# mLSTM's q, k, gate and value projections as seven half-size products each

## The chip, the cores and the metric

The kernel runs on one core of a Trainium2 chip. The metric is the device time of one execution in microseconds. Before the change the median of three runs is 1254.02 us (1248.43 to 1255.01).

## What is computed

One decoder layer on x of 1024 tokens x 1024 features, in float32. A normalised x goes through one projection `w_in`. It feeds eight dilated attention heads and four mLSTM heads; their outputs meet in `w_out`, and a gated convolutional FFN of width 2816 follows. What matters here is the part of the projection that feeds the mLSTM heads:

```python
def _hybrid_mixer(h, w_in, ...):
    proj = h @ w_in
    aq, ak, av, mq, mk, mv, mo, mig, mfg = jnp.split(proj, SPLITS, axis=-1)
    ...
    mqk = jax.nn.silu(_causal_dwconv(jnp.concatenate([mq, mk], axis=-1), mlstm_conv_w, mlstm_conv_b))
    mq, mk = jnp.split(mqk, 2, axis=-1)
    ...
    hm = _mlstm_chunkwise(ml_heads(mq), ml_heads(mk) * (MLSTM_HEAD_DIM ** -0.5), ml_heads(mv), log_i, log_f)
    hm = _rmsnorm(hm, ...)
    hm = jax.nn.sigmoid(mo.astype(jnp.float32)) * hm
```

q, k, the gate `mo` and the values `mv` are 512 columns each; the gate unit also carries the eight columns of the input and forget gates.

## The kernel before

Every float32 product is three matmuls of rounded parts: high by high, high by low, low by high (`mm3`, L327). An operand is therefore split into a high part (a rounded copy, on ACT or VectorE) and a low part (a subtraction, on VectorE or POOL).

The program is one long instruction list for each engine, written out by a planner. `Clock` (L29) holds a modelled time for each engine, `Lanes` (L171) a list of generators with priorities. A generator yields what it needs (tiles, free pages of SBUF, free PSUM banks, a condition), and the planner goes on with the first lane whose needs are met at TensorE's modelled time. The order on each engine is fixed by this plan; on the chip each instruction waits for its semaphores in that order. The planner's `dma` (L291) counts loads on SP's queue one after the other and does not count transfers that other engines issue.

x is kept as sixteen pages, `xh` and `xl`, high and low part of eight blocks of 128 features by 1024 tokens. The first three q and k units are multiplied while x arrives (the loop at L504), 18 matmuls for each block. `project` (L648) then goes through `order` (L404): the units m (q or k of a head, `ml_conv` behind each), g (gate), v (mLSTM values), a (attention values) and h (q and k of an attention head). An m or h unit is 2 halves of tokens x 8 blocks x 3 matmuls of 512 columns. A g or v unit is 8 token blocks x 8 feature blocks x 3 matmuls of 260 or 256 columns. The gate stays in SBUF (`sg`), as do q and k (`qk`). `mlstm` (L810) runs a head's recurrence over eight chunks when its q, k, values and gates are there. In the same stretch run the attention lanes `scores`, `trans` and `values` (L943 to L1039).

`stacks` (L912) prepares an attention head: it scales the product by R, splits it, and swaps halves of 64 partitions between three pages with four transfers SBUF to SBUF (`move`, L306, on SP's queue):

```python
        move(kS[lo, A], q2[up, A])
        move(kS[up, A], q1[up, A])
        move(q1[up, A], q2[lo, A])
        move(q2[up, A], q1[lo, A])
```

The FFN already uses seven products of half size for each 2 x 2 block product. The sums of its weights are made in DRAM by `sums` (L788): a copy issued on ACT's queue, then an add issued on POOL's queue (`accum_op`), each of 5.6 MB for the upward weights, planned from 70 us on at intervals of 55 us.

Of the kernel before, what the change touches and what calls it, by code (L numbers as in the profile page):

```python
# [223 lines left out]
def tile_hybrid_layer(ctx, tc, xT, x, w_t, w_v, w_g, w_o, w_uq, w_dq, params, fnw, c_id, c_att, c_sel,  # L224
# [14 lines left out]
    usum = {p: dram.tile([DFF, 512], F32, name=f"usum{p}") for p in (3, 5, 6, 7)}  # L239
    hpark = [dram.tile([128, 1024], F32, name=f"hpark{i}") for i in range(8)]  # L240
# [65 lines left out]
    def move(dst, src):  # L306

        nc.sync.dma_start(f32(dst), f32(src))
        t = max(clk.eng.get("dma", 1.7), clk.ready(src), clk.last(dst))
        clk.eng["dma"] = t + 0.7  # L310
        for a in (dst, src):
            n = a.tensor.name
            clk.acc[n] = max(clk.acc.get(n, 0.0), clk.eng["dma"] + 2.0)
        for k in clk.cells(dst):
            clk.wr[k] = clk.eng["dma"] + 2.0
            clk.weng[k] = "dma"
# [19 lines left out]
    class Feed:  # L336
# [35 lines left out]
        def split_next(self):  # L372
            n, raws = self.raw.pop(0)
            res = []
            for raw, s in zip(raws, self.units[n]):
# [4 lines left out]
                e = dve if hold or clk.eng.get("pool", 0.0) > clk.eng.get("dve", 0.0) + PB else pool  # L380
                e.tensor_tensor(lo[:, :w], raw[:, :w], f32(hi[:, :w]), op=OP.subtract)
# [22 lines left out]
    order = "m3 g0 g1 v0 m4 m5 v1 m6 m7 a0 h0 h1 h2 h3 a1 h4 h5 h6 h7"  # L404
    for o in order.split():
        n = int(o[1])
        if o[0] == "m":
            unit("ml", n, [w_t[n]])
        elif o[0] == "h":
            unit("att", n, [w_t[8 + n]])  # L410
        elif o[0] == "g":
            unit("g", n, [w_g[n, 0], w_g[n, 1]])
        elif o[0] == "v":
            unit("mv", n, [w_v[2 + n, 0], w_v[2 + n, 1]])
        else:
            unit("av", n, [w_v[n, 0], w_v[n, 1]])
    feed = Feed(units, 1, 6)
# [23 lines left out]
    xh = [page(f"xh{k}", F32R) for k in range(8)]  # L441
    xl = [page(f"xl{k}", F32R) for k in range(8)]
    w0 = [page(f"w0r{c}") for c in range(3)]
    w0h = [page(f"w0h{c}", F32R) for c in range(3)]
    w0l = [page(f"w0l{c}", F32R) for c in range(3)]
    raws = {}
    H = [slice(0, 512), slice(512, 1024)]

    def load_x(k, hf):
        if hf == 0:  # L450
            raws[k] = page("xr")
        dma(raws[k][:, H[hf]], xT[k * 128:(k + 1) * 128, H[hf]])

    def load_w0(k, n):
        sl = slice(k * 128, (k + n) * 128)
        for c in range(3):
            dma(w0[c][:, sl], w_t[c][:, sl])

    def load_nat(i):
        t = page("xnat")  # L460
        dma(t[:, :D], x[i * 128:(i + 1) * 128, :])
        raws["n", i] = t

    def split_x(k, hf):
        wn = pr[:, P_XN + k:P_XN + k + 1]
        xr = raws[k]
        act.activation(xh[k][:, H[hf]], xr[:, H[hf]], AF.Copy, scale=wn)
        dve.scalar_tensor_tensor(xl[k][:, H[hf]], xr[:, H[hf]], wn, f32(xh[k][:, H[hf]]), op0=OP.mult,
                                 op1=OP.subtract)
        if hf:  # L470
            free(raws.pop(k))

    def split_w0(k, n):
        sl = slice(k * 128, (k + n) * 128)
        for c in range(3):
            dve.tensor_copy(w0h[c][:, sl], w0[c][:, sl])
            pool.tensor_tensor(w0l[c][:, sl], w0[c][:, sl], f32(w0h[c][:, sl]), op=OP.subtract)

# [29 lines left out]
    for k in range(8):  # L508
# [4 lines left out]
        elif k + 2 < 8:  # L513
            if k == 2:
                load_w0(4, 4)
            load_x(k + 2, 0)
            load_x(k + 2, 1)
        if k == 4:
            feed.fetch(0)
            dma(ident, c_id)  # L520
            for i in range(4):
                load_nat(i)
# [1176 lines left out]
```

## Time and profile before

| | us |
|---|---|
| median of 3 runs | 1254.02 |
| lowest, highest | 1248.43, 1255.01 |
| the profiled execution | 1251.1 |
| its span, first to last instruction | 1249.3 |
| TensorE busy | 1221.0 |
| VectorE busy | 868.2 |
| ACT busy | 576.5 |
| POOL busy | 300.0 |

Busy times are unions of an engine's instructions; waiting and issuing transfers are not counted. The ends of matmuls are modelled, so the pace from one start to the next says more than the busy time. Nearly all instructions carry line L153, a helper that records them; they are told apart by the names of what they write and read. The granted clock of TensorE over the span is 0.99 of full speed.

### The profile page before, as it was taken

Reading aid. Unit: us, or ns where it says so; the run is one execution under the profiler, and the core shown is the slowest. Engines: PE = TensorE matmul, PEld = TensorE weight load, DVE = VectorE, ACT = ScalarE, POOL = GpSimd, SP = SyncE. Lnnn points to the kernel's source line nnn. Section 1 sums busy time; section 2 is a strip of 40 time slices with the busy share of each in tenths; the row PEclk is TensorE's granted clock in tenths of the full one; section 3 lists DMA queues with packets and bytes.
Section 4 is the critical chain, followed back from the end, with each engine's and each line's share of the span. In section 5 each row is a group of like instructions: output and inputs, shape, how many; then the busy total and the mean of one; then the engine's idle time right before and its main releaser. Section 6 shows DMA issues by size and latency. Waiting matters only on the chain. (4 is left out here: it accounts for less than half of the span.)

```text
span 1249.3 us, 17498 instructions
## 1 busy us (share of the span) xinstructions
PE 1221.0 (98%) x6366; PEld 1031.3 (83%) x6366; DVE 868.2 (69%) x1622; ACT 576.5 (46%) x1146; POOL 300.0 (24%) x213
## 2 busy tenths in 40 slices
PE   9999999999999699999999999999999999999997
PEld 6899898988998598788878888888888888888886
DVE  6733472657784487635799877777776878877865
ACT  4454554536562366334654344343343444343553
POOL 3420132121103103121133332323322222424002
PEclk9999999999999799999999999999999999999999
DMA  9460656668493759823663865546634279433334
GB/s 332 174 213 25 147 163 231 144 152 251 129 193 94 269 178 233 214 86 142 143 212 133 243 222 164 188 161 195 179 107 152 82 288 409 148 102 90 97 97 147
DMA packets 66366, 216.41 MB, mean 173 GB/s; under 512 B 7268, under 2 KB 8804, under 8 KB 61288
## 3 DMA queue, kind: packets, MB, share of 16 engines
q1 hardware_dynamic: 61032, 146.09, 34.8%
q0 software_dynamic: 4352, 34.60, 13.7%
q10 hardware_dynamic: 896, 34.60, 8.1%
q8 instruction: 50, 0.82, 0.3%
q14 instruction: 36, 0.29, 0.1%
HBM read 182.76 MB, written 93.32 MB: 221 GB/s over the span
## 5 line engine op out<-in xcount | busy, mean ns | idle before, releaser
L153 PE MATMUL bank<-xb,W 128*128 128x512 f32 x1848 | 431.1, 395 | 2.6 <-POOL W L153 2.1
L153 PEld LDWEIGHTS bank<-xb,W 128*128 128x128 f32 x1848 | 347.8, 188 | 84.9 <-POOL W L153 2.5
L153 PE MATMUL bank<-B,A 128*128 128x512 f32 x924 | 214.0, 394 | 0.0
L153 PEld LDWEIGHTS bank<-B,A 128*128 128x128 f32 x924 | 173.6, 188 | 40.2
L153 POOL TENSOR_TENSOR W<-ur,W 128x512 fp32r<-128x512 f32 x82 | 107.2, 1329 | 278.4 <-ACT W L153 258.0
L153 ACT ACTIVATE ua<-bank,pr 128x512 f32<-128x512 f32 x84 | 63.0, 777 | 168.9 <-DVE bank L153 161.0
L153 DVE SCALAR_TENSOR_TENSOR ua<-bank,pr,ua 128x511 f32<-128x511 f32 (+1 forms) x168 | 125.4, 746 | 15.9 <-ACT ua L153 12.9
L153 DVE TENSOR_TENSOR bank<-bank,ut 128x512 f32<-128x512 f32 x84 | 58.6, 697 | 38.2 <-PE bank L153 37.2
L153 ACT ACTIVATE W<-ur 128x512 fp32r<-128x512 f32 x133 | 78.5, 623 | 5.9 <-DMA ur<-in_w_uq_dram 3.2
L153 ACT ACTIVATE A<-g 128x512 fp32r<-128x512 f32 x76 | 47.3, 627 | 71.9 <-DVE g L153 47.2
L153 DVE CUSTOM_DVE_ANT_0 P<-bank,matt 128x512 f32<-128x512 f32 (+3 forms) x96 | 50.7, 552 | 19.6 <-PE bank L153 17.5
L153 ACT ACTIVATE P<-P,nmx 128x128 f32<-128x128 f32 (+3 forms) x64 | 49.5, 773 | 29.3 <-DVE nmx L153 29.0
L153 DVE TENSOR_TENSOR ut<-ut,bank 128x512 f32<-128x512 f32 x66 | 45.0, 681 | 19.5 <-PE bank L153 19.0
L153 DVE TENSOR_TENSOR B<-br,B 128x512 fp32r<-128x512 f32 x67 | 50.4, 755 | 11.5 <-ACT B L153 11.4
L153 DVE TENSOR_TENSOR PT<-bank,PT 128x512 fp32r<-128x512 f32 (+1 forms) x80 | 48.3, 630 | 8.2 <-ACT PT L153 7.9
L153 PE MATMUL bank<-kS,q 128*128 128x512 f32 (+3 forms) x192 | 42.4, 354 | 10.9 <-DMA q<-q 10.9
L153 POOL TENSOR_TENSOR A<-g,A 128x512 fp32r<-128x512 f32 x17 | 23.2, 1372 | 122.2 <-ACT A L153 122.2
L153 DVE TENSOR_TENSOR W<-ur,W 128x512 fp32r<-128x512 f32 x72 | 49.9, 701 | 2.2 <-ACT W L153 1.5
L153 DVE TENSOR_TENSOR A<-g,A 128x512 fp32r<-128x512 f32 x60 | 41.7, 700 | 13.6 <-ACT A L153 13.2
L153 DVE TENSOR_TENSOR hq<-hq,bank 128x512 f32<-128x512 f32 x56 | 34.9, 681 | 20.9 <-PE bank L153 20.9
L153 ACT ACTIVATE B<-br 128x512 fp32r<-128x512 f32 x69 | 42.4, 619 | 14.9 <-DMA br<-in_w_dq_dram 10.1
L153 ACT ACTIVATE PT<-bank 128x512 fp32r<-128x512 f32 (+1 forms) x71 | 36.5, 547 | 24.9 <-PE bank L153 23.4
(357 smaller groups left out, 2467.2 us busy)
## 6 DMA issues: line engine op xcount, KB each, us to landing
usum<-in_w_uq_dram POOLq DMA_DIRECT2D x4, 5632.0 KB, 34.9
ur<-usum SPq DMA_DIRECT2D x88, 256.0 KB, 4.5
ur<-in_w_uq_dram SPq DMA_DIRECT2D x66, 256.0 KB, 4.6
usum<-in_w_uq_dram ACTq DMA_DIRECT2D x2, 5632.0 KB, 21.1
usum<-usum ACTq DMA_DIRECT2D x2, 5632.0 KB, 22.8
tsum<-in_w_dq_dram POOLq DMA_DIRECT2D x4, 2816.0 KB, 18.1
gp<-ua SPq DMA_DIRECT2D x22, 512.0 KB, 2.9
g<-gp SPq DMA_DIRECT2D x22, 512.0 KB, 7.6
```

What stands on the lines that cost most here:

```text
L153: r = f(*a, **k)
```

## The change

Each of the four projections is cut in two along features and in two along tokens or columns, and its four quarter results are put together from seven products of half size. x becomes blocks `xp[1]` to `xp[7]` of 512 features by 512 tokens: the quarters for products 1 to 3, sums for 5 to 7 and 4, made by `x_half` and `x_sums`. The weight sums for products 3, 5, 6 and 7 are made in DRAM by `p_sums`, by a copy on ACT's queue and an add on POOL's queue each, at times of the plan that `p_plan` lists. `products` runs the steps: q and k of four heads with products 1 and 2, the gate with 1 and 2, the gate's rest in the order 6, 7, 5, 3, 4, q's and k's rest for two heads at a time, then the values. `m_evac` and `t_evac` combine the results on VectorE. q and k after the convolution (`qkp`) and the gate (`gpark`) are stored to DRAM on POOL's queue and loaded again by `mlstm`. `project` keeps the attention units alone, and starts behind the last product; the second token half of the first four x blocks is loaded and split again for it (`x_last`, `xp[8]`). The half swaps of `stacks` go to POOL's queue (`put`). The FFN's upward sums move from 70 us, every 55, to 130 us, every 40.

```diff
+    gpark = dram.tile([128, 8, 512], F32, name="gpark")
+    msum = {p: dram.tile([512, 512], F32, name=f"msum{p}") for p in (3, 5, 6, 7)}
+    gsum = {p: dram.tile([128, 1040], F32, name=f"gsum{p}") for p in (3, 5, 6, 7)}
+    vsum = {p: dram.tile([128, 1024], F32, name=f"vsum{p}") for p in (3, 5, 6, 7)}
+    qkp = [dram.tile([128, 1024], F32, name=f"qkp{i}") for i in range(8)]
...
-    def move(dst, src):
-        nc.sync.dma_start(f32(dst), f32(src))
...
+    def put(dst, src):
+        nc.gpsimd.dma_start(dst, src)
+        t = max(clk.eng.get("pool", 0.0), clk.ready(src), clk.last(dst))
+        clk.eng["pool"] = t + 1.0
         for a in (dst, src):
             n = a.tensor.name
-            clk.acc[n] = max(clk.acc.get(n, 0.0), clk.eng["dma"] + 2.0)
-        for k in clk.cells(dst):
-            clk.wr[k] = clk.eng["dma"] + 2.0
...
-    order = "m3 g0 g1 v0 m4 m5 v1 m6 m7 a0 h0 h1 h2 h3 a1 h4 h5 h6 h7"
+    order = "a0 h0 h1 h2 h3 a1 h4 h5 h6 h7"
...
-    feed = Feed(units, 1, 6)
+    feed = Feed(units, 1, 6, wait=lambda: "plain" in flags)
...
+    xs = [page(f"xs{k}") for k in range(8)]
+    xp = {p: {} for p in range(1, 9)}
+    wn = lambda k: pr[:, P_XN + k:P_XN + k + 1]
+    rest = (6, 7, 5, 3, 4)
+    psteps = [("m", h, p) for p in (1, 2) for h in range(4)] + [("g", 0, 1), ("g", 0, 2)]
+    psteps += [("g", 0, p) for p in rest]
+    psteps += [("m", h, p) for i in (0, 2) for p in rest for h in (i, i + 1)]
+    psteps += [("v", 0, p) for p in (1, 2) + rest]
+    praw, pw = {}, {}
+    pused = [0]
+    sumt = {}
...
     dma(pr, params)
-    load_x(0, 0)
-    load_w0(0, 1)
...
-    rst_pg = page("rst")
-    rst = rst_pg[0:4, :S]
-    for k in range(8):
...
+    for k in (0, 4, 1, 5, 2, 6, 3, 7):
+        dma(xs[k][:, U], xT[k * 128:(k + 1) * 128, U])
+    def p_load():
+        n = 8
+        while n < len(psteps):
+            m = psteps[n][0] == "m"
+            yield need(pg=1, keep=2, cond=lambda: n < max(pused[0] + (5 if m else 3), 11) and summed(n))
+            if m:
+                yield need(pg=1, keep=2, cond=lambda: summed(n + 1))
+            t = page("pr")
+            for j in range(1 + m):
+                src = psrc(*psteps[n + j])
+                dma(t[:, H[j]] if m else t[:, :src.shape[-1]], src)
+                praw[n + j] = t
+            n += 1 + m
...
+    def p_side():
+        for n, (u, h, p) in enumerate(psteps):
+            m = u == "m"
+            yield need(cond=lambda: n in praw and n < pused[0] + (4 if m else 3 if n < 11 else 2))
+            r = praw.pop(n)
...
+                    yield from split(t, r[:, H[i]])
+                if i:
+                    free(r)
...
+    def x_half(p, k, hf, raw):
+        s_ = xs[k][:, H[hf]]
+        if raw:
+            yield need(s_, pg=1)
+            t = page(f"xp{p}", F32R)
+            act.activation(t[:, L], s_, AF.Copy, scale=wn(k))
+            yield need(t[:, L])
+            dve.scalar_tensor_tensor(t[:, U], s_, wn(k), f32(t[:, L]), op0=OP.mult, op1=SUB)
+            xp[p][k % 4] = t
+            yield need(t, cond=lambda: len(xp[2]) == 4)
+            act.activation(s_, s_, AF.Copy, scale=wn(k))
+        else:
+            yield need(s_)
+            act.activation(s_, s_, AF.Copy, scale=wn(k))
+            if p:
+                flags.add(("x", k, hf))
+                yield need(s_, pg=1, keep=2, cond=lambda: len(xp[5]) > k - 4 and calm())
+                t = page(f"xp{p}", F32R)
+                yield from split(t, s_)
+                xp[p][k % 4] = t
+        flags.add(("x", k, hf))
...
+    def x_sums(f):
+        yield need(cond=lambda: all(("x", k, hf) in flags for k, hf in ((f, 0), (f, 1), (f + 4, 0), (f + 4, 1))) and calm())
+        lo, up = xs[f], xs[f + 4]
+        yield need(lo, up, pg=1)
+        tm = page("xt")
+        two(lo[:, U], lo[:, U], lo[:, L], SUB)
+        yield need(lo)
+        two(tm[:, L], up[:, U], lo[:, U], SUB)
+        for p, src in ((6, tm[:, L]), (7, tm[:, U]), (5, lo[:, U]), (4, up[:, L])):
+            if p == 7:
+                two(tm[:, U], tm[:, L], lo[:, L], SUB)
+                two(up[:, L], up[:, L], tm[:, L], SUB)
+            yield need(src, pg=1, cond=calm)
+            t = page(f"xp{p}", F32R)
+            yield from split(t, src)
+            xp[p][f] = t
+            if p in (5, 7):
+                free(lo if p == 5 else tm)
+            before = {6: 6, 7: 7, 5: 3, 4: 3}[p]
+            yield need(cond=lambda: len(xp[before]) == 4)
+        free(up)
...
+    def p_sums(u, quarters, into, plan_):
+        for t, to, src, add in plan_:
+            yield need(cond=lambda: clk.eng.get("pe", 0.0) > t)
+            src = quarters[src] if isinstance(src, tuple) else into[src]
+            if add:
+                nc.gpsimd.dma_start(into[to], src, accum_op=ADD, max_dma_last_dim=8192)
+            else:
+                nc.scalar.dma_start(into[to], src)
+            if add:
+                sumt[u, to] = clk.eng["pe"] + 10.0
+    def p_plan(c, a, c6, a6, c3, a3):
+        return ((c, 5, (1, 0), 0), (c, 7, (1, 0), 0), (a, 5, (1, 1), 1), (a + 1, 7, (0, 0), 1), (c6, 6, 5, 0),
+                (a6, 6, (0, 0), 1), (c3, 3, 6, 0), (a3, 3, (0, 1), 1))
+    ij = [(i, j) for i in range(2) for j in range(2)]
+    lanes.add(p_sums("g", {k: w_g[k] for k in ij}, gsum, p_plan(11, 17, 23, 29, 35, 41)), 0.1)
+    lanes.add(p_sums("m", {k: w_mq[k].rearrange("h p c -> (h p) c") for k in ij}, msum, p_plan(20, 30, 40, 48, 57, 65)), 0.2)
+    lanes.add(p_sums("v", {k: w_v[2 + k[0], k[1]] for k in ij}, vsum, p_plan(36, 44, 52, 60, 68, 74)), 0.3)
...
+        put(qkp[2 * h + isk], a[:, :S])
...
+    def m_evac(h, p, b):
+        if p == 1:
+            yield need(b, pg=1 - h % 2)
+            if h % 2 == 0:
+                run[h] = page("ut")
+            t = run[h // 2 * 2][:, H[h % 2]]
+            act.activation(t, b, AF.Copy)
+            run["m", h] = t
+            freebank(b)
+            return
+        yield need(b, cond=lambda: ("m", h) in run)
+        t = run["m", h]
+        yield need(t, pg=1 if p in (2, 7) else 0)
+        if p == 2:
+            zt[h, 0] = page("z0")
+            dve.tensor_tensor(zt[h, 0][:, L], b, t, op=ADD)
+            flags.add(("C", h, 0, 0))
+            flags.add(("at", h, 2))
+            freebank(b)
+            return
+        yield need(cond=lambda: ("at", h, {6: 2, 7: 6, 5: 7, 3: 5, 4: 5}[p]) in flags)
+        if p == 6:
+            dve.tensor_tensor(t, t, b, op=SUB)
+        elif p == 7:
+            zt[h, 1] = page("z1")
+            dve.tensor_tensor(zt[h, 1][:, L], t, b, op=ADD)
+        elif p == 5:
+            dve.tensor_tensor(zt[h, 0][:, U], t, b, op=SUB)
+            dve.tensor_tensor(zt[h, 1][:, U], b, zt[h, 1][:, L], op=SUB)
+            flags.add(("C", h, 1, 1))
+            if ("at", h ^ 1, 5) in flags:
+                free(run[h // 2 * 2])
+        elif p == 3:
...
+                    put(gpark[:, 2 * i:2 * i + 2, :], sg[i][:, :S].rearrange("p (t c) -> p t c", t=2))
...
+    def products():
+        for n, (u, h, p) in enumerate(psteps):
+            if u != "m" and p == 2:
+                yield need(pg=2)
+                dst = sg if u == "g" else va
...
+                for t in va[-2:]:
+                    pool.memset(t[:, :1032].rearrange("p (t h j) -> p t h j", t=2, h=4)[:, :, :, 128:129], 1.0)
+            yield need(cond=lambda: n in pw)
+            w = pw[n]
+            if u == "m":
+                yield need(*w, bk=1, kb=2)
+                b = bank("fg")
+                for f in range(4):
+                    yield need(cond=lambda: f in xp[p])
+                    x_ = xp[p][f]
+                    yield need(x_)
+                    fs, fl = slice(f * 128, (f + 1) * 128), slice(512 + f * 128, 512 + (f + 1) * 128)
+                    mm3(b, w[0][:, fs], w[0][:, fl], x_[:, L], x_[:, U], f == 0, f == 3)
+                lanes.add(m_evac(h, p, b), 3)
+            else:
...
+                    if u == "g" or j % 2 == 0:
+                        yield need(*w, bk=1, kb=2)
+                        b = bank("fg")
+                    o = b[:, :c] if u == "g" or j % 2 == 0 else b[:, 256:512]
+                    for f in range(4):
+                        yield need(cond=lambda: f in xp[p])
+                        x_ = xp[p][f]
+                        yield need(x_)
+                        fs = slice(f * c, (f + 1) * c)
+                        mm3(o, x_[:, j * 128:(j + 1) * 128], x_[:, 512 + j * 128:512 + (j + 1) * 128], wh[:, fs],
+                            wl[:, fs], f == 0, f == 3)
+                    if u == "g" or j % 2:
+                        lanes.add(t_evac(u, p, j if u == "g" else j // 2, b), 3)
+            free(*pw.pop(n))
+            pused[0] = n + 1
+            if u == "v" and p in (4, 5, 6, 7):
+                free(*xp.pop(p).values())
+            if n == len(psteps) - 3:
+                flags.add("plain")
+        flags.add("products")
...
-    lanes.add(sums(70, 55, uq, usum, ((5, (1, 0), 0), (5, (1, 1), 1), (6, 5, 0), (6, (0, 0), 1), (3, 6, 0),
+    lanes.add(sums(130, 40, uq, usum, ((5, (1, 0), 0), (5, (1, 1), 1), (6, 5, 0), (6, (0, 0), 1), (3, 6, 0),
...
     def mlstm(h):
-        yield need(cond=lambda: 2 * h in qk and 2 * h + 1 in qk and "urow" in G and ("mv", h // 2) in flags)
-        q, k = qk.pop(2 * h), qk.pop(2 * h + 1)
+        yield need(pg=2, keep=5, cond=lambda: 2 * h in qk and 2 * h + 1 in qk and "plain" in flags
+                   and (h == 0 or ("begun", h - 1) in flags))
+        q, k = page("q"), page("k")
+        for i, t in enumerate((q, k)):
+            dma(t[:, :S], qkp[2 * h + i])
+        yield need(q, k, pg=1, keep=5, cond=lambda: "urow" in G and "v" in flags)
+        flags.add(("begun", h))
         urow = G["urow"]
-        yield need(q, k, pg=1, keep=5)
...
+        dma(yp[:, :S].rearrange("p (t c) -> p t c", t=8), gpark[:, :, h * 128:(h + 1) * 128])
...
-        move(kS[lo, A], q2[up, A])
-        move(kS[up, A], q1[up, A])
-        move(q1[up, A], q2[lo, A])
-        move(q2[up, A], q1[lo, A])
+        put(f32(kS[lo, A]), f32(q2[up, A]))
+        put(f32(kS[up, A]), f32(q1[up, A]))
+        yield need(kS)
+        put(f32(q1[up, A]), f32(q2[lo, A]))
+        put(f32(q2[up, A]), f32(q1[lo, A]))
```

## Rows read from the trace of the kernel before

**Rows 1.** the page: each engine's busy us, share and instructions

```profile
PE 1221.0 (98%) x6366; PEld 1031.3 (83%) x6366; DVE 868.2 (69%) x1622; ACT 576.5 (46%) x1146; POOL 300.0 (24%) x213
```

**Rows 2.** TensorE's waits, whole span: us in total, times, longest

```profile
PE bank L153 <- DMA q<-q: 10.9, 2, 8.9
...
PE bank L153 <- DVE W L153: 0.4, 1, 0.4
```

**Rows 3.** groups of instructions (busy us, mean ns), then two stretches (header above)

```profile
L153 PE MATMUL bank<-xb,W 128*128 128x512 f32 x1848 | 431.1, 395 | 2.6 <-POOL W L153 2.1 <-DVE W L153 0.4
...
core 0: us, PE busy (x) PEld busy (x) DVE busy (x) ACT busy (x) POOL busy (x), PEclk, DMA share, GB/s
80.00:100.00 20.00, 20.00 (x169) 20.00 (x169) 0.00 (x0) 4.32 (x15) 0.00 (x0) 1.00 0.67 215
...
56.00:66.00 10.00, 10.00 (x86) 10.00 (x85) 10.00 (x8) 6.59 (x8) 2.13 (x1) 1.00 0.15 52
```

**Rows 4.** TensorE in order of time, 8 to 20 us: start, us, instructions

```profile
10.97 0.94 PE L153 MATMUL bank<-xh,w0h 128*128 128x512 f32 x3 [1.26 <-DVE w0h L153]
17.66 0.51 PE L153 MATMUL bank<-xh,w0l 128*128 128x512 f32 x1 [0.63 <-POOL w0l L153]
```

**Rows 5.** stretches, same columns: two early ones, a copy, adds, adds with loads

```profile
0.00:5.00 5.00, 3.81 (x9) 1.34 (x10) 0.76 (x6) 2.21 (x3) 0.66 (x5) 1.00 0.52 159
20.00:40.00 20.00, 20.00 (x88) 16.19 (x87) 14.79 (x17) 9.63 (x15) 9.84 (x6) 1.00 1.03 413
75.00:80.00 5.00, 5.00 (x44) 5.00 (x44) 0.00 (x0) 2.58 (x5) 4.09 (x5) 1.00 1.06 364
605.00:615.00 10.00, 10.00 (x45) 8.12 (x44) 9.79 (x18) 6.56 (x13) 1.57 (x1) 1.00 1.01 210
485.00:515.00 30.00, 28.23 (x176) 24.30 (x174) 19.31 (x53) 14.30 (x32) 0.00 (x0) 1.00 1.03 247
```

**Rows 6.** groups by shape: VectorE whole span, then ACT from 0 to 165

```profile
L153 DVE TENSOR_TENSOR ut<-ut,bank 128x512 f32<-128x512 f32 x66 | 45.0, 681 | 19.5 <-PE bank L153 19.0
L153 DVE TENSOR_TENSOR OT<-bank,osum 64x256 f32<-64x256 f32 x32 | 13.3, 414 | 7.5 <-ACT osum L153 6.6
L153 DVE SCALAR_TENSOR_TENSOR xl<-xr,pr,xh 128x512 fp32r<-128x512 f32 x16 | 14.7, 954 | 7.7 <-ACT xh L153 7.7
...
L153 ACT ACTIVATE w1h<-wr 128x1040 fp32r<-128x1040 f32 x2 | 2.1, 1074 | 2.9 <-DMA wr<-in_w_g_dram 2.9
```

**Rows 7.** the stretch from 0 to 163; groups of it by shape

```profile
0.00:163.00 163.00, 158.52 (x1030) 140.57 (x1031) 84.35 (x126) 83.80 (x181) 42.93 (x32) 0.99 0.58 180
...
L153 DVE SCALAR_TENSOR_TENSOR mqk<-mz,pr,mqk 128x1023 f32<-128x1023 f32 x5 | 10.5, 2109 | 0.0
L153 DVE SCALAR_TENSOR_TENSOR mqk<-mz,pr,mqk 128x1021 f32<-128x1021 f32 x4 | 5.1, 1274 | 0.0
```

**Rows 8.** in order of time, 405 to 435 us; then the stretch at its end

```profile
408.34 0.50 ACTq L799 DMA_DIRECT2D usum<-in_w_uq_dram  x1
...
427.74 0.48 PE L153 MATMUL bank<-kS,q 128*128 128x128 f32 x1 [8.89 <-DMA q<-q]
430.22 1.65 PE L153 MATMUL bank<-kS,q 128*128 128x128 f32 x5 [2.00 <-DMA q<-q]
...
430.00:435.00 5.00, 4.78 (x13) 4.09 (x14) 2.61 (x12) 0.49 (x2) 0.00 (x0) 0.50 0.19 76
```

**Rows 9.** DMA issues: KB each, us to landing; POOL's issue; fifth head in time

```profile
usum<-in_w_uq_dram POOLq DMA_DIRECT2D x4, 5632.0 KB, 34.9
kS<-q SPq DMA_DIRECT2D x16, 256.0 KB, 3.6
...
L796 POOL DMA_DIRECT2D usum<-in_w_uq_dram x4: 1132/1172/1291, 133.4 to 480.4; - x4
...
397.80 1.10 SPq L308 DMA_DIRECT2D q<-q  x2
...
403.71 0.98 PE L153 MATMUL bank<-kS,q 128*128 128x128 f32 x6
```

More of the change, by code (lines that the diff above doesn't have):

```diff
@@ new lines, in calm, with stats @@
+    def calm():
+        return max(clk.eng.get("dve", 0.0) - 2.5, 1e-9)
+    for k in range(4):
+        lanes.add(x_half(1, k, 0, True), 2.0)
+    for k in range(4, 8):
+        lanes.add(x_half(2, k, 0, True), 2.1)
+    for k in range(4):
+        lanes.add(x_half(0, k, 1, False), 2.2)
+        lanes.add(x_half(3, k + 4, 1, False), 2.25)
+        lanes.add(x_sums(k), 2.3)
+    def stats():
+        for i in range(8):
+            yield need(pg=1, keep=4, cond=lambda: len(xp[2]) == 4 and len(stat_done) > i - 3)
+            t = page("xnat")
+            dma(t[:, :D], x[i * 128:(i + 1) * 128, :])
+            lanes.add(stat(i, t), 2.6)
+        dma(ident, c_id)
+        dma(tri, c_tri)
+        yield need(ident, cond=lambda: len(stat_done) == 8)
+        dve.tensor_scalar(ss, ss, 1.0 / D, EPS, op0=OP.mult, op1=OP.add)
+        pool.tensor_tensor(rn, ss, half, op=OP.pow)
+        yield need(rn, pg=1)
+        R.append(page("R"))
+        for hf in range(2):
+            yield need(bk=1)
+            pR = bank()
@@ L619, in tile_hybrid_layer @@
     va = []
-    vap = []
     av = {}
@@ new lines, in x_last @@
+    def x_last():
+        for f in range(4):
+            yield need(pg=2, cond=lambda: 5 not in xp)
+            r = page("xr")
+            dma(r[:, L], xT[f * 128:(f + 1) * 128, U])
+            t = page("xp8", F32R)
+            yield need(r)
+            act.activation(t[:, L], r[:, L], AF.Copy, scale=wn(f))
+            yield need(t[:, L])
+            dve.scalar_tensor_tensor(t[:, U], r[:, L], wn(f), f32(t[:, L]), op0=OP.mult, op1=SUB)
+            free(r)
+            xp[8][f] = t
+    lanes.add(x_last(), 2.3)
@@ L648, in project @@
     def project():
+        yield need(cond=lambda: "products" in flags)
         for n, (kind, arg) in enumerate(plan):
@@ L874, in mlstm @@
             free(ET, ST)
-        free(q, k, vap[h])
+        free(q, k)
+        flags.add(("vused", h))
+        if all(("vused", j) in flags for j in range(4)):
+            free(*va)
         yield need(nmp, pg=1)
@@ L943, in scores @@
     def scores():
+        yield need(pg=1, cond=lambda: "products" in flags)
+        matt = page("matt")
+        dma(matt[:, :S], c_att)
+        yield need(matt)
         for h, pr_ in pairs:
@@ L1239, in tile_hybrid_layer @@
     gp = [dram.tile([128, 1024], F32, name=f"gp{k}") for k in range(NK)]
-    L, U = slice(0, 512), slice(512, 1024)
-    ADD, SUB = OP.add, OP.subtract
-    def two(out_, a, b, op):
-        end = {}
-        for n in ("dve", "pool"):
-            c = clk.cost(n, "tensor_tensor", [out_], [a, b], {})
-            end[n] = clk.start(n, c, [out_], [a, b]) + c
-        (pool if end["pool"] + 0.3 < end["dve"] else dve).tensor_tensor(out_, a, b, op=op)
-    def split(t, src):
-        copy(t[:, L], src)
-        yield need(t[:, L])
-        two(t[:, U], src, f32(t[:, L]), SUB)
     def blocks_ready(hf):
```

428 lines of the change are left out of this document (239 added, 189 removed).

## Prediction

> **What bounds the kernel now.** I read the busy shares first, then what TensorE waits for, then the stretches. TensorE is busy 98% of the span, every other engine 69% or less [rows 1]. That alone proves little, since the ends of matmuls are modelled, so the second view counts: all waits of TensorE that the trace names, ten rows, come to about 22 us, and 10.9 us of them are two waits for the half-swapping transfers of one attention head [rows 2]. The third view is the pace. 1848 matmuls of 512 columns with no others between take 431.1 us, 0.233 us each; in a stretch of value products 169 matmuls of 256 columns fill 20 us, 0.118 us each; in a gate stretch 86 fill 10 us, some of them cut by its edges, 0.12 us for 260 columns [rows 3]. So the kernel's time is its number of matmul columns plus some 25 us of holes. A matmul that goes saves its whole pitch, if what is left stays fed.
>
> **The change, part by part.** *Products.* Before, the eight q and k units take 2 halves x 8 blocks x 3 = 48 matmuls of 512 each (384), the two gate units 8 x 8 x 3 = 192 of 260 each (384), the two value units as many of 256. After, q and k are 4 head groups x 7 products x 4 blocks x 3 = 336, gate and value 7 x 4 x 4 x 3 = 336 each. 48 go of each kind: 48 x 0.233 + 48 x 0.12 + 48 x 0.118 = 22.6 us. All of it is on TensorE, so all of it is on the path. Transposes, attention, output and FFN keep their counts.
>
> *The start.* Before, 144 products need 33.5 us and run from 5 to 42 us: 3.5 us of waits, seen as the two gaps at 11 and 17.7 us [rows 4]. The new start asks for the same first 256 KB of x and 64 KB of weights; I let its own waits cost the same 3.5 us.
>
> *The sums of weights.* Each of gate, q/k and value gets four copies (ACT's queue) and four adds (POOL's queue) in DRAM: 2.1 + 4.2 + 2.1 = 8.4 MB copied and 8.4 MB added, planned between 11 and 74 us. Rates, each from a stretch with that traffic alone: loads 413 GB/s, a copy 364, an add 210, all three at a full DMA share; an add with loads beside it moves 247 in all [rows 5]. The eight p1 and p2 steps of q and k keep TensorE from 5 to 5 + 96 x 0.233 = 27.4 us. By then the first gate weights must be in. In front of them on SP's queue lie 24 half blocks of 256 KB, with the gate page 6.8 MB: 16.5 us, and some 3 us more because the first 5 us moved only 159 GB/s [rows 5]. The sums planned before 27 us bring copies of 3.7 MB (10.2 us) and adds of 1.06 MB (5.1 us). Together the engines need until 35 us, and the split of the page takes 1.07 us on ACT and, at twice 0.68, about 1.4 on VectorE [rows 6]: some 10 us late. The lower bound is 0, if the loads win the sharing; the upper is +20, if the q/k adds (2.1 MB, 10 us) also get in front. The early stretch of before is nearest: with loads alone it waited 3.5 us at a full share. I take +7, range -3 to +23. Two blocking points add to the upper end: a copy waits in ACT's stream for the add it reads, with evacuations and splits behind it, and an add waits in POOL's stream for its copy, with weight splits and the new stores behind it.
>
> *VectorE.* Added in the first 163 us, at about 0.7 us for 512 columns [rows 6]: evacuations of q/k 28 x 0.69, less nothing, because the 16 multiplications by R remain (19 us); of gate and value 28 x 0.42 (as for 256 columns) + 14 x 0.69 = 21; x splits and sums 20 x 0.7 + 16 x 0.69 + 4 x 0.95, less 8 x 0.95 = 21; 12 more pages of weight splits at 1.4 = 17. That is 78 us, and the last two convolutions, some 12 us, come in, while about 25 us of gates and recurrences move behind. VectorE has 84 us and POOL 43 us there now [rows 7]; with POOL's time at half, 106 + 78 + 12 - 25 = 171 us of VectorE's work in about 160. POOL can take 30 or 40 of it. VectorE stays under the bound as a mean, but the q/k stretch holds 48 us of convolutions beside 17 of evacuation in 56 us, and it must spill into the value stretch. An operation can get longer there: the convolution's step of 1023 columns takes 2.11 us in the mean of this stretch, its step of 1021 columns 1.27 [rows 7]. I take +3, range 0 to +15 if that cover fails.
>
> *Attention's transfers.* The four half swaps of a head go from SP's queue to POOL's. Now, at 408.34 us ACT issues a 5.6 MB copy; TensorE then stands 8.89 and 2.00 us for swaps, and has half its clock from 430 to 435 us, 1.2 GHz after 10 us of standing still: 10.9 + 2.5 = 13.4 us [rows 8]. A swap lands in 3.6 us normally [rows 9]. The FFN's sums move to 130 us and every 40 us, so copies and adds cover the attention stretch as densely as now. Best case: no swap meets one, -13. Worst: two heads sit behind whole adds, 34.9 us each [rows 9], less 6 us from the last swap to the scores (397.80 to 403.71 for the fifth head) [rows 9]: 2 x 29 - 13.4 = +44. The nearest row is that one head's stall, which a new spacing moves but does not remove: 0.
>
> *Parking and reloads.* q, k and gate make 6.3 MB of stores and as many loads in 1249 us; POOL's issues, 12 stores and 32 swaps at about 1.2 us, as its adds take now [rows 9], are 53 us on an engine that is 24% busy. The recurrences ask for them when two value products are still to run, and a0, h0 to h2 lie behind as cover. Nothing; a few us, if a load meets a 5.6 MB copy.
>
> Sum: -22.6 + 7 + 3 + 0 = -12.6. The profiled execution took 1251.1 us (1.8 around its span), 2.9 below the median: 1238.5 on its scale, 1241.4 on the median's. I say 1240. All terms at their ends at once would give 26 less or 72 more.
>
> **The rivals.** *All fed, 1226.* The gate weights come in time and the new spacing spares the swaps half of their 13.4 us: 1254 - 22.6 - 6 = 1226. For it: the adds are needed late, the value sums only after 124 us. Against it: the full DMA share of the early stretch even without sums [rows 5].
>
> *Swaps queue behind adds, 1266, slower.* A POOL queue that takes swaps after a 5.6 MB add in the order of issue lets them land when the add has. Place: the heads from h3 on, whose scores follow the last swap as closely as the fifth head's. Price: 20 us for each of two heads, 40 in place of 13.4, so 1240 + 27 = 1266. It decides from one head that waits 26 us in all. The adds fill 35 of each 80 us, so of five heads two are exposed. Against it: heads stacked early have other attention work in front of them. The Trainium skill, "DMA: Bandwidth & Descriptors", section "Queues, rings and completion order", says that a DMA engine takes its queue rows in turn, packet by packet, and consumes one row's descriptors in ring order. The stretch with an add and loads agrees on the turns (247 GB/s against 210); no row shows a transfer behind an add in its own queue. By that rule a swap on SP's queue shares with an add, and one on POOL's waits for its end: it is this rival.
>
> *The sums starve the loads throughout, 1256.* Up to the last gate product (67 us): 8.4 MB of adds 40 us, 8.4 of copies 23, 14.2 MB of loads 34, 97 us against some 75: 22 us late instead of 7, so 1240 + 15 = 1255 to 1257.
>
> *VectorE sets the pace, 1252.* +15 instead of +3.
>
> *The change doesn't cut the columns.* Excluded by the counts above.
>
> **How the numbers follow.** Forecast 1240 (its own range 1232 to 1248): 0.42. All fed: 0.22. Swaps behind adds: 0.17. Sums starve: 0.11. VectorE: 0.08. About 0.5%, 6.3 us, is what a measurement of this kernel can tell from no change: 1247.7 to 1260.3. Faster: 0.39 of the forecast's share and 0.22, 0.61. Same: 0.03 of the forecast, 0.08, and 0.07 of the starving case, 0.18. Slower: 0.17 and 0.04, 0.21. The range 1224 to 1266 leaves out the better end of the second case and the worse end of the third, under 0.2.
>
> **What would show it.** Right: 336 products each; a TensorE gap of 5 to 10 us before the first gate product at about 27 us; VectorE over 80% busy from 40 to 160 us; the first out-projection product some 10 us earlier than now. Wrong upward: no gap there and TensorE's waits under 15 us in all. Wrong downward: a wait on kS or q1 of over 15 us beside an add, or TensorE waiting for summed weights after 70 us.

## The result, and the profile after

The kernel after takes 1369.71 us (median of 4 runs, 1368.39 to 1371.01), the kernel before 1251.94 (median of 4 beside them): a ratio of 1.094, with an interval of 1.091 to 1.098. The change costs 117.8 us; 1240 was forecast, 1266 was the upper end.

The page of after, the rows that answer to [rows 1], and the granted clock and the DMA share in 40 slices of 34 us (tenths):

```profile
PE 1228.4 (90%) x6222; PEld 1031.6 (75%) x6222; DVE 934.9 (68%) x1759; ACT 604.6 (44%) x1197; POOL 266.8 (19%) x239
...
PEclk9789988889798999799999999999999999999999
DMA  9987579465979377922154756665563358733324
```

144 matmuls fewer, as the change says, and TensorE's busy share falls from 98% to 90%. No other engine is near its bound. The clock drops in some of the first 17 slices and nowhere behind them. TensorE's waits answer to [rows 2] (us in total, times, longest); two rows of POOL's and one of SP's queue stand below them:

```profile
PE bank L153 <- DMA q<-q: 43.5, 6, 19.0
PE bank L153 <- DVE rows L153: 17.8, 2, 17.3
PE bank L153 <- ACT pwh L153: 17.6, 2, 14.1
PE bank L153 <- DVE y L153: 10.9, 2, 10.2
PE bank L153 <- ACT PT L153: 8.5, 1, 8.5
...
POOL q L313 <- DMA kS<-q: 77.1, 7, 33.0
POOL gsum L675 <- DMA gsum<-gsum: 21.8, 2, 17.7
...
SPq L297 <- DMA y<-gpark: 29.2, 1, 29.2
```

Some 22 us of waits have become well over 100, and most end at work fed by a transfer: the swaps, the gates' rows behind reloads of x, a summed gate weight, the parked gate. The issues with their median us from issue to landing, last column, name the slow ones (compare [rows 9]):

```profile
usum<-in_w_uq_dram POOLq DMA_DIRECT2D x4, 5632.0 KB, 37.1
kS<-q POOLq DMA_DIRECT2D x16, 256.0 KB, 12.6
pr<-gsum SPq DMA_DIRECT2D x4, 520.0 KB, 25.2
q<-qkp SPq DMA_DIRECT2D x4, 512.0 KB, 23.6
y<-gpark SPq DMA_DIRECT2D x4, 512.0 KB, 18.9
```

The account of the 118 us: I gave every matmul the pitch of its width in an undisturbed stretch (0.232 us for 512 columns, 0.118 for 256, as in [rows 3]), called it a wait where the distance to the next start exceeds that by more than 0.25 us and 1.3 pitches, and put all smaller excesses into the column of the slow clock, which is therefore an upper bound for it. From the first matmul (at 1.2 us) to the first product of the FFN (at 592.9 us before, at 711.4 after):

| us | matmuls at their pitch | waits | slow clock | sum |
|---|---|---|---|---|
| before | 563.7 | 20.3 | 7.7 | 591.7 |
| after | 541.1 | 139.8 | 29.2 | 710.1 |
| after less before | -22.6 | +119.5 | +21.5 | +118.4 |

From there to the last matmul both take the same (649.5 and 649.1). The first column counts matmuls at the forecast's own pitch, so its -22.6 confirms the count of the products and not yet a gain. Waits take almost seven times as much. They cost twice: in four stretches around the longest ones the granted clock (the column before the DMA share) is 0.76 to 0.81 of 2.4 GHz in the mean, that is, part of the time at 1.2, and the DMA engines are full:

```profile
0.00:80.00 80.00, 52.30 (x237) 40.76 (x238) 35.35 (x61) 38.30 (x65) 10.36 (x14) 0.81 0.98 313
205.00:243.00 38.00, 15.70 (x127) 14.92 (x126) 18.01 (x21) 6.78 (x11) 1.16 (x1) 0.79 1.03 257
335.00:369.00 34.00, 15.31 (x98) 13.44 (x96) 10.24 (x25) 11.18 (x53) 3.81 (x5) 0.76 1.04 237
546.00:582.00 36.00, 15.94 (x99) 14.20 (x98) 16.87 (x49) 11.62 (x28) 4.44 (x5) 0.76 1.01 247
```

Each of the last three holds one 5.6 MB add: issued at 204.95, 331.67 and 535.46 us, landed at 243.03, 367.79 and 579.08. The middle one in order of time (start, us, instructions; in brackets the idle time before it and what ended it):

```profile
330.57 1.13 POOL L313 DMA_DIRECT2D kS<-q  x2 [15.99 <-DVE mC L153]
331.67 1.27 POOL L1087 DMA_DIRECT2D usum<-in_w_uq_dram  x1
336.62 1.10 POOL L313 DMA_DIRECT2D q<-q  x2 [3.68 <-DMA kS<-q]
...
369.36 0.45 PE L153 MATMUL bank<-kS,q 128*128 128x128 f32 x1 [19.05 <-DMA q<-q]
```

The first two swaps of a head leave before the add and land in 3 to 5 us. The other two leave 5 us behind it and land at 369.23 and 370.40, the first of them 1.4 us after it. TensorE stands 19.05 us for them. The Trainium skill, "DMA: Bandwidth & Descriptors", section "Queues, rings and completion order", says that a ring's descriptors are consumed in ring order. The trace agrees: all eight swaps issued on POOL's queue while an add was in flight landed after it, while a load of 512 KB issued on SP's queue at 331.94, 0.3 us after one of these adds, landed at 336.97.

The startup has its own hole, where no upward sum runs yet:

```profile
45.09 0.80 POOL L675 DMA_DIRECT2D gsum<-in_w_g_dram  x1 [17.70 <-DMA gsum<-gsum]
45.62 1.98 POOL L675 DMA_DIRECT2D msum<-in_w_mq_dram  x2
...
52.32 3.00 SPq L297 DMA_DIRECT2D pr<-gsum  x3
...
70.06 1.07 ACT L153 ACTIVATE pwh<-pr 128x1040 fp32r<-128x1040 f32 x1 [14.28 <-DMA pr<-gsum]
...
71.18 0.58 PE L153 MATMUL bank<-pwh,xp 128*128 128x260 f32 x1 [14.10 <-ACT pwh L153]
```

Gate product 6 needs a sum two links deep (copy, add, copy, add). POOL stood 17.7 us for the second copy, the last add landed at 52.27, and the 520 KB load, issued at once, took 17.7 us beside two 1 MB adds.

### The profile page after: what moved, and what is told of

The parts are those of the page before. It is cut to its first block, busy times and chain, and to the rows that moved or that the text cites. A ratio compares the mean times of both kernels' runs of the same rounds, so it can differ in the third digit from the quotient of the medians.

```text
span 1369.2 us, 17560 instructions
## 1 busy us (share of the span) xinstructions
PE 1228.4 (90%) x6222; PEld 1031.6 (75%) x6222; DVE 934.9 (68%) x1759; ACT 604.6 (44%) x1197; POOL 266.8 (19%) x239
## 3 DMA queue, kind: packets, MB, share of 16 engines
q1 hardware_dynamic: 66952, 151.35, 31.9%
## 5 line engine op out<-in xcount | busy, mean ns | idle before, releaser
L153 PE MATMUL bank<-pwh,xp 128*128 128x260 f32 (+1 forms) x448 | 90.9, 303 | 24.7 <-ACT pwh L153 17.6
L153 PEld LDWEIGHTS bank<-pwh,xp 128*128 128x128 f32 x448 | 77.2, 209 | 26.1 <-ACT pwh L153 18.2
L153 DVE TENSOR_TENSOR bank<-bank,ut 128x512 f32<-128x512 f32 (+1 forms) x96 | 64.8, 674 | 39.4 <-PE bank L153 38.4
L153 PE MATMUL bank<-xp,pw 128*128 128x512 f32 x336 | 83.3, 407 | 4.4 <-DVE pw L153 3.6
L153 PE MATMUL bank<-kS,q 128*128 128x512 f32 (+3 forms) x192 | 45.9, 372 | 45.0 <-DMA q<-q 43.5
L153 PEld LDWEIGHTS bank<-xp,pw 128*128 128x128 f32 x336 | 64.6, 194 | 22.5 <-ACT ut L153 3.0
L153 PE MATMUL bank<-pwl,xp 128*128 128x260 f32 (+1 forms) x224 | 68.6, 306 | 9.9 <-DVE pwl L153 8.3
L153 PEld LDWEIGHTS bank<-kS,q 128*128 128x128 f32 x192 | 33.8, 207 | 50.7 <-issue 43.1
L153 DVE TENSOR_TENSOR ut<-ut,bank 128x512 f32<-128x512 f32 (+1 forms) x82 | 53.6, 654 | 20.3 <-PE bank L153 19.8
L153 PE MATMUL bank<-PT,av 128*128 128x256 f32 (+1 forms) x320 | 50.8, 292 | 10.7 <-ACT PT L153 8.5
## 6 DMA issues: line engine op xcount, KB each, us to landing
usum<-in_w_uq_dram ACTq DMA_DIRECT2D x2, 5632.0 KB, 22.4
usum<-usum ACTq DMA_DIRECT2D x2, 5632.0 KB, 21.5
```

The source lines that it names most:

```text
L153: r = f(*a, **k)
```

## The experiments

Each variant ran once, beside one run of the kernel before on the same chip (1250.1 to 1251.4). The four runs of the kernel after lie within 2.6 us, those of the kernel before within 6.6, so a difference of a few us from one run isn't told from none. A is the theory that the cost is the meeting of small transfers with the sums; the main rival is that the load on the DMA engines costs by its bytes.

**Which sums.** The three parts without them:

```diff
 e1: p_sums issues nothing; psrc gives w_mq[1, 0, h], w_g[1, 0], w_v[3, 0] for p = 3, 5, 6, 7
 e2: sums issues nothing into usum; upward() reads w_uq[1, 0] for p = 3, 5, 6, 7
 e3: both
```

> The changed kernel without the sums of the gate, q/k and value weights: no copy and no add for them, and products 3, 5, 6 and 7 read an unsummed quarter (this part of the computation is left out). Everything else keeps its place in the plan. Theory A (transfers that the sums and the FFN's sums put in front of what TensorE needs next): the waits up to about 105 us go, 27 us and some 8 us of slow clock, while the FFN's sums still collide: 1370 - 35 = 1335, range 1315 to 1350. Rival B (VectorE or ACT set the pace of the seven products): within 10 us of 1370, and TensorE still waits for pwh and pwl before 105 us. Rival C (the swaps' queue alone): within 10 us of 1370 too, but with the early waits gone.

> The changed kernel without the sums of the FFN's upward weights: no 5.6 MB copy or add, the upward products 3, 5, 6 and 7 read an unsummed quarter (left out). Theory A: the waits that lie beside one of these eight transfers go, 17.4 us for the gates, 10.3 for the gate's reload, 19.2, 5.9 and 17.5 for swaps, 8.7 and some 12 more, 91 us, and some 15 us of slow clock: 1370 - 105 = 1265, range 1250 to 1285. Rival B: 1340 or more, since VectorE's work is as it was. Rival C (swaps alone): 1370 - 43 - 8 = 1320.

> Both left out: no sums of projection weights and no upward sums. Theory A: only the products and what was there before remain. Warm work of TensorE up to the output stage 463 us, of the rest 724, with waits and slow clock of some 15 and 7 us as before, and 2 us around the span: 1211, range 1203 to 1225. Rival B: above 1240, with TensorE waiting for VectorE's or ACT's results in the seven products' stretch.

Measured: 1331.35, 1264.22, 1223.77. Against 1369.7 the small sums cost 38.4 us, the upward sums 105.5, both together 145.9. They hardly overlap. Without any of them the kernel is 27.6 us faster than the kernel before, but that one still makes its upward sums: against e5 below, which leaves them out there, it is 11.7 us faster. In e3 the reloads land in 4.0 to 4.5 us (issues) and TensorE's longest row of waits totals 3.5:

```profile
q<-qkp SPq DMA_DIRECT2D x4, 512.0 KB, 4.0
y<-gpark SPq DMA_DIRECT2D x4, 512.0 KB, 4.5
```

```profile
PE bank L153 <- DVE pwl L153: 3.5, 2, 1.8
```

**The same upward sums in the kernel before.**

```diff
 e5 (before): sums issues nothing into usum; upward() reads w_uq[1, 0] for p = 3, 5, 6, 7
```

> The kernel before without the copies and adds that form the upward weights' sums (usum); upward products 3, 5, 6 and 7 read an unsummed quarter, so that part of the computation is left out. The same transfers cost the kernel after 105 us. Theory A (a sum costs where a small transfer that TensorE is about to need meets it; in the kernel before only one set of swaps did, 8.89 + 2.00 us of waits): 1236 to 1246 against 1251. Theory B (moving these bytes costs the same in any kernel, by the load on the DMA engines): 1146 to 1200.

Measured: 1235.50, half a microsecond below A's range. The 45 MB that cost 105.5 us in the kernel after cost 14.6 in the kernel before. Bytes alone are not the price.

**The two things that the change did to them: the timetable and the swaps' queue.** Each alone and both, in the kernel before:

```diff
 e11: -    lanes.add(sums(70, 55, uq, usum, ...
      +    lanes.add(sums(130, 40, uq, usum, ...
 e12: -        nc.sync.dma_start(f32(dst), f32(src))        # move(): attention's swaps
      +        nc.gpsimd.dma_start(f32(dst), f32(src))
 e14: both
```

> The kernel before with its upward sums issued from 130 us, 40 us apart, as the change has them, in place of 70 and 55; same queues, same bytes. Its sums cost 14.6 us at their old times. Theory A (the cost is the meeting of a sum with a transfer that TensorE needs at once, and the denser timetable stands where attention's swaps are, on another queue than the adds): 1252 to 1270. Theory D (the change's 105 us come of the timetable above all): 1290 to 1350.

> The kernel before with the swaps of attention's halves issued on POOL's queue, behind the adds, as the change has them, in place of SP's; same order on every other engine, sums at their old times. Theory A (on one queue a swap lands after the add ahead of it): swaps issued within 30 us behind an add wait for it; with four adds and eight heads two to three of them meet one, 10 to 20 us of TensorE's time each less what other work covers: 1262 to 1290. Theory D (the queue does not matter): 1246 to 1253.

> The kernel before with both edits: upward sums from 130 us, 40 us apart, and the swaps of attention's halves on POOL's queue behind the adds. Alone they cost 4.8 and 6.8 us. Theory A (what counts is a swap that is issued behind an add in flight, and the new timetable puts adds between the swaps of a head): more than the sum of the two, 1270 to 1310. Theory E (the meetings matter little in the kernel before, whose order has the swaps well ahead of the scores that use them): 1257 to 1266, the sum of the two or less.

Measured: 1254.83 (+4.8), 1256.82 (+6.8), 1277.07 (+26.2): together more than twice the sum of the two. The first two differences are too small to be told from none by one run each, and e12 lies between its two ranges; 26.2 is clear. In e12 no swap happened to be issued while an add was in flight on its queue; in e14 two heads were. The first of them in order of time (the add landed at 293.0, the swaps at 295.0 and 296.2):

```profile
258.39 1.15 POOL L796 DMA_DIRECT2D usum<-in_w_uq_dram  x1
...
276.78 1.14 POOL L308 DMA_DIRECT2D kS<-q  x2 [5.71 <-PE bank L153]
296.45 1.01 POOL L308 DMA_DIRECT2D q<-q  x2 [18.53 <-DMA kS<-q]
...
299.38 0.45 PE L153 MATMUL bank<-kS,q 128*128 128x128 f32 x1 [11.28 <-DMA q<-q]
```

So in the kernel before timetable and queue together bring 26 us, of the 91 by which the upward sums cost more in the kernel after. No run isolates the rest: the reloads and the new order of the kernel's parts are left for it, and for the reloads only the waits above speak.

**The same two in the kernel after, from the other side.**

```diff
 e4:  the four put(...) of stacks() issue on nc.sync in place of nc.gpsimd
 e16: -    lanes.add(sums(130, 40, uq, usum, ...
      +    lanes.add(sums(165, 45, uq, usum, ...
```

> The changed kernel with the four half swaps of each attention head issued on SP's queue again, at the same places of the plan; all sums stay. Theory A with the queue as a part of it: a swap no longer lies behind an add on POOL's queue, so the waits of 19.2 and 17.5 us beside adds shrink to a few us, the one of 5.9 us beside a copy stays: 1370 - 30 - 5 of clock = 1335, range 1325 to 1350. Rival (the transfers are slow from sharing the 16 engines, not from their place in a queue): within 8 us of 1370.

> The kernel after with the upward sums issued from 165 us, 45 us apart, in place of 130 and 40; whole transfers, same queues and packets. The wait of the gates for the reloads of x and the copies at 188 us go, since no sum runs there; the swaps still meet adds, others than before. Theory A: 1335 to 1362 against 1369.7. Theory F (which transfers happen to meet decides, and moving the whole timetable by a third of a sum's spacing leaves as many meetings): 1362 to 1385.

Measured: 1351.55 and 1304.48. The queue gives back 18 us, less than half of the 43.5 that the swaps' waits total and outside both ranges, A's by 1.6 us. A wait of 15.9 us at ACT's P comes up instead; ACT, with P behind, stands there 28.55 and 5.77 us for loads of `w_out` that share the engines with the next add. Of the eight swaps issued on SP's queue in an add's flight, five landed before the add did, after 3.1 to 16.4 us; on POOL's queue in the kernel after none of eight had. So it is the place in the queue that holds a swap until the add's end, and sharing the engines costs besides.

The timetable alone (35 us later, and 45 apart in place of 40) gives 65 us, far more than either theory had said. It does so without removing all the meetings. At 371.34 us the swaps of a head leave 4 us behind an add again, and land 30 us later; but in that stretch TensorE had value products of attention to do, and was busy all the time at full clock (order of time; then the stretch, busy us of PE, PEld, DVE, ACT, POOL, granted clock, DMA share, GB/s):

```profile
367.64 1.23 POOL L1087 DMA_DIRECT2D usum<-in_w_uq_dram  x1
371.34 1.05 POOL L313 DMA_DIRECT2D q<-q  x2 [2.48 <-DMA kS<-q]
```

```profile
367.60:400.80 33.20, 33.20 (x274) 32.58 (x273) 23.51 (x62) 17.31 (x38) 2.44 (x5) 1.00 0.99 206
```

So a meeting costs what the work that TensorE still has leaves uncovered. e16's gap at the gates fell from 17.4 to 13.0 us, and the holes at 350, 413, 512 and 562 us went; one of 13.6 at 482 came, where the swaps of another head stand behind an add.

**Packets and pieces.** In the kernel after, copies in packets of 4 KB; upward sums in four row quarters; both, with e4's swaps; and eighths with adds in 4 KB packets (on top of e10, below):

```diff
 e6:  nc.scalar.dma_start(..., src, max_dma_last_dim=4096)        # p_sums and usum
 e7:  for i in range(4): dma_start(flat(into[to])[rs], src[rs], ...); t += dt / 4
 e8:  e4, e6 and e7
 e15: e10 with range(8), adds with max_dma_last_dim=4096
```

> The kernel after with the copies (not the adds) of the gate, value, q/k and upward sums cut into packets of 4 KB in place of 33 to 65 KB; everything else and the order on every engine as before this edit. Theory A1 (a DMA engine takes turns between queues packet by packet, so that a load of 4 KB packets gets under a tenth of an engine beside 45 KB packets): the loads that met copies land in about half the time, the waits at 57, 188, 293, 413 and 512 us shrink, those behind adds (350, 562) stay: 1325 to 1352 against 1369.7. Theory B (bytes alone count: engines are full, whatever the packets): 1364 to 1375. Should copies of small packets themselves take much longer, the waits for sums grow: up to 1390.

> The kernel after with each copy and add of the upward weights' sums cut into four row quarters, issued a quarter of the old spacing apart (10 us of the planner's time), same bytes, same queues. Theory A (a small transfer waits for what is left of one transfer of 22 to 37 us, on POOL's queue by order): a swap or load now meets a quarter of it (6 to 10 us), and the waits at 350 and 562 us (19.2 and 17.5 us, and the waits of swaps behind them) fall to under 8 us each, that at 224, 293 and 413 by half: 1315 to 1345 against 1369.7. Theory B (load on the DMA engines): 1360 to 1375, since the bytes and the time in which they go are the same.

> The kernel after with three edits together: upward sums in quarters, copies in 4 KB packets, and the swaps of attention's halves on SP's queue. Theory A: the stage with attention keeps little of its 76 us of waits (20 to 35), the startup keeps its add-bound wait for the gate's sums (14 to 30 us): 1290 to 1320. Theory B (load): 1345 to 1360, what moving the swaps alone gave (1351.6).

> The kernel of the run with all edits and later sums (1279.35) with the upward sums in eighths in place of quarters and the adds in packets of 4 KB in place of 8 KB. Theory A (the longest wait of a small transfer is one piece, and its share of an engine goes by packet sizes): 1262 to 1276. Theory B (what is left is load on the engines): 1277 to 1290, more if adds in smaller packets take longer.

Measured: 1344.05, 1321.79, 1306.99, 1279.89. The same bytes in smaller packets give 25.7 us, in smaller transfers 47.9; by the rival neither should give more than 10. The quarters are also spread over the time between two sums, and e7 does not separate that from their size. The packets show in the copies' queue (packets, MB, share of the engines), of after and then of e6, and in e6's issues of a load and of the first two swaps of a head:

```profile
q10 hardware_dynamic: 1280, 43.03, 8.8%
```

```profile
q10 hardware_dynamic: 8384, 43.03, 8.9%
```

```profile
pr<-gsum SPq DMA_DIRECT2D x4, 520.0 KB, 14.2
kS<-q POOLq DMA_DIRECT2D x16, 256.0 KB, 7.6
```

From 34 KB a packet in the mean to 5, at the same share of the engines, and the summed gate weight lands in 14.2 us in place of 25.2, the swaps in 7.6 in place of 12.6. With eighths nothing more comes (1279.89 against 1279.35), and the rival's range was hit. That does not show that the meetings have stopped: the longest of TensorE's waits in e15 is one, a parked gate whose load of 512 KB takes 31.2 us beside adds in eighths (in e10 the longest wait on `y` is 8.6):

```profile
PE bank L153 <- DVE y L153: 20.0, 2, 17.9
```

**The startup.** The value sums' times later; the q/k sums behind the gate's besides; and both among all the other edits:

```diff
 e9:  p_plan(36, 44, 52, 60, 68, 74) -> p_plan(72, 80, 88, 96, 104, 110)      # value
 e17: e9, p_plan(20, 30, 40, 48, 57, 65) -> p_plan(33, 37, 43, 48, 57, 65)    # q/k
 e10: e8, e9 and sums(165, 45, ...)
 e18: e10 and e17
```

> The kernel after with the copies and adds of the value weights' sums issued at 72 to 110 us of the planner's time in place of 36 to 74, nothing else. Theory A (the startup is short of DMA throughput: the engines are busy all of the first 80 us, and 4.2 MB of the 16.8 MB that the small sums write leave that stretch): the gate weights' loads land sooner, the waits at 57, 77 and 102 us (14.3, 2.5, 1.8) shrink, 1352 to 1364 against 1369.7. Theory C (the gate sums wait for their own chain of copy, add and load, each behind the q/k sums on its queue, and the value sums stand behind those anyway): within 4 us of 1369.7.

> The kernel after with the q/k sums' first copies and adds put behind the gate's (33 and 37 us of the planner's time in place of 20 and 30, third copy at 43 in place of 40) and the value sums at 72 to 110 us as in the run that moved those alone (1365.1). Theory A (the gate's sum for product 6 and its load are held up by the two 1 MB adds issued with them): the wait for that product falls from 8.5 us to under 4 us, the one before it by 2 or 3, and no new wait for the q/k sums comes up before 100 us: 1350 to 1360. Theory C (the chain of five transfers itself and eight loads of natural x on SP's queue decide): 1361 to 1368. If the q/k sums come too late, new waits at 90 to 110 us: up to 1375.

> The kernel after with quarters, copies in 4 KB packets and the swaps on SP's queue (together 1307.0), and besides the value sums at 72 to 110 us and the upward sums from 165 us, 45 us apart, in place of 130 and 40. Theory A (what is left is small transfers that meet sums: at 216 us the last reloads of x, at 52 to 67 the gate's weights): 1270 to 1298. Theory B (a later start only moves the collisions on to attention's swaps): 1298 to 1325. The kernel without any sums, 1223.8, is the floor.

> The run with quarters, 4 KB copies, swaps on SP's queue and later upward and value sums (1279.35) with the q/k sums behind the gate's as well. Theory A: the two waits of 7.3 and 7.7 us before the first summed gate product shrink by half, 1268 to 1276. Theory C: 1276 to 1284. The kernel before stands at 1251.

Measured: 1365.08, 1361.52, 1279.35, 1279.13. In e17 the load of the summed gate weight is the one that no longer meets the q/k adds: it takes 3.6 us in place of 17.7 (11.9 in e9), and the wait for product 6 is gone, as A has it; the time is the other theory's. Two others stand in its place, one for the norm, one for the next gate weight, which now lands beside the q/k adds:

```profile
56.52 1.97 PE L153 MATMUL bank<-ident,rn 128*128 128x128 f32 x8 [7.85 <-POOL rn L153]
...
85.92 0.59 PE L153 MATMUL bank<-pwh,xp 128*128 128x260 f32 x1 [7.68 <-ACT pwh L153]
```

e9 lies between the two ranges. Order gave 8 us of the startup's 38; the rest moved. On top of all other edits it gave nothing (e18 against e10, as theory C had it). All edits together leave 1279, 28 us above the kernel before. No version here beats it with all sums made.

## Why the prediction was wrong, point by point

What failed are the terms for transfers. The sums of weights, put at +7, cost 38.4; attention's transfers and the reloads, put at 0 and "nothing", turned upward sums that cost 14.6 us before into 105.5.

*The products* were right as a count: 336 of q/k, 672 of gate and value. That all of the 22.6 us would reach the time was not: e3 against e5, both without upward sums and e3 without any others, gives 11.7. By the account above TensorE's waits before the FFN are then some 15 us in e3 against 7 in e5. *VectorE* had +3 as a guess. In e3 it is busy 103.6 of the 120 us from 40 to 160, as forecast, and TensorE still 118.9 of them; in the kernel after, with its holes, VectorE is busy 66% there.

The gap before the first gate product is there (4.8 us), at 36 us and not at 27, and not for the reason that was given: that product's weights had landed at 24.3 us. The 96 matmuls ahead of it had ended only at 36.8 us (at 31.9 in e3), a start that the forecast had put at the same waits as before. ACT stood behind a copy in its stream until the add that the copy reads had landed, and the split of the weights stood behind that copy. This was named as a point of blocking and had no price:

```profile
38.62 0.48 ACTq L677 DMA_DIRECT2D gsum<-gsum  x1
39.15 1.07 ACT L153 ACTIVATE pwh<-pr 128x1040 fp32r<-128x1040 f32 x1 [6.27 <-DMA gsum<-in_w_g_dram]
```

Both signs of "wrong downward" came: 19.05 us for a swap beside an add, 14.10 us for a summed weight at 71 us.

*The sums of weights, +7 (range -3 to +23),* measured 38.4 in e1. The step that failed priced only the arrival of the first, unsummed gate weights at 27 us. The sums themselves have a deadline, product 6 at 57 us, at the end of a chain of five transfers that each share full engines; and the loads of x in its natural layout, 4 MB on SP's queue from 20 to 43 us, were not in that term. The wait of POOL for a copy was named as a point of blocking and given no price; it stood 17.7 us. The rival that starves the loads had the right place with +15 for its price.

*Attention's transfers, 0 (-13 to +44).* Here the forecast took the nearest row, one stalled head, and said that a new spacing moves it without removing it. Measured are 43.5 us of TensorE's waits for swaps, against 10.9 before. In the kernel before the forecast holds for the spacing (+4.8) and for the queue (+6.8), each alone. Together they are +26.2 there. That is the rival of swaps that queue behind adds, priced at +27 and given 0.17. Against it stood that heads stacked early have other work in front; the 19 us at 350 us are the very first head's, which has none.

*Parking and reloads, "nothing; a few us".* TensorE's longest waits behind reloads are 17.3 and 10.2 us. The term was priced by bytes and by issues on an idle engine. What counted was that every reload is a new small transfer with a reader close behind it, on engines that a 5.6 MB sum fills: q from 4.0 to 23.6 us, the gate from 4.5 to 18.9, and the reloads of a quarter of x, which the prediction did not price and behind which the gates' operations stood in VectorE's order (TensorE's 17.3 us). The change added small transfers on the path, and moved the sums to where they are. e16 and e7 show with 65 and 48 us what the timetable and the cutting of the sums are worth; what the reloads alone cost is not shown, since no run leaves them out.

*The clock* was priced at 2.5 us, for one stall. It took up to 21.5, because there were five waits of 10 to 19 us where before had none.

*Rivals taken one at a time.* By these runs the case is two of them with the unpriced reloads on top. Each was on the list or in a subordinate clause; they add, since they lie in different stretches (e1 and e2: 38.4 + 105.5 against 145.9 for both).

With the small sums at their measured price, 1240 was out of reach. The floor without sums (1223.8), with the upward sums at their price in the kernel before (14.6) and the small ones at theirs (38.4), comes to 1276.8, an estimate from these runs; e10 reached 1279.35. That the small sums' 38 us cannot be brought under what the products save is not shown: e17 moved their waits rather than removed them, and later gate products, on more pages, were not tried.

## What to carry to other kernels

Price a bulk transfer by whom it meets, not by its bytes alone: for each small transfer on the path ask what is ahead of it on its own queue, what shares its engines, and what work its reader has left until it lands. An edit that parks data adds such transfers, and one that moves a timetable changes whom they meet, so the two must be priced together. Cut bulk into pieces and small packets and keep it off the queue of what is urgent before counting what was saved in arithmetic.

## What the hardware showed that I had not expected

A DRAM-to-DRAM copy in packets of some 34 KB holds up transfers on other queues far more than the same copy in 4 KB packets. Four swaps of 256 KB on POOL's queue, issued while a 5.6 MB copy of ACT's queue was in flight, took 14.3 to 17.1 us in the kernel after and landed within 1.5 us of the copy's end; in e6 twelve of them took 2.9 to 9.1. Not everything gains: a parked gate's load beside a copy took 18.9 and 19.1. The copy in large packets is itself the faster one (22.4 against 28.0 us for the copies of upward weights).

On POOL's queue behind a 5.6 MB add the first swap landed 0.6 to 2.2 us after the add in six cases (two each in the kernel after, e14 and e16), where the same transfer alone takes 2.8 to 3.6 in all. And a timetable of eight transfers that starts 35 us later and is 5 us wider between them was worth 65 us of the kernel.
